# Low parts of up's and gate's left factors subtracted on DVE instead of POOL, with one low part of the operand forms, in a two-layer hybrid trunk

## The chip, the cores and the metric

The kernel runs on one core of a Trainium2 chip. The metric is the device time of one execution in microseconds (us), the median of the runs of a kernel. The engines have the profile's names: PE multiplies matrices, DVE and POOL do elementwise arithmetic, ACT applies functions and copies, SP issues the transfers. Each engine takes its instructions strictly in the order of its own queue.

## What is computed

Two layers over 1024 prompt frames and 64 frames of a running stream (1088 tokens, width 1024). Layer 0 mixes tokens with a state-space model and a gated linear unit, layer 1 with forgetting attention; each is followed by a convolutional feed-forward block. Cut from the reference:

```python
def conv_ffn(x, hist, w_up, w_gate, conv_w, conv_b, w_down):
    a = x @ w_up                                   # 1024 -> 2816
    a_pad = jnp.concatenate([hist.astype(a.dtype), a], axis=1)
    conv = a_pad[:, 0:l] * conv_w[0]
    for j in range(1, CONV_WIDTH):
        conv = conv + a_pad[:, j:j + l] * conv_w[j]
    h = jax.nn.gelu(conv + conv_b) * (x @ w_gate)
    return h @ w_down, a_pad[:, -(CONV_WIDTH - 1):]
```

## The kernel before

Activations stand transposed, as eight tiles of 128 features by 1088 tokens, in chunks of 272 tokens. Every fp32 matrix is split into a high part (a rounded copy, made by ACT) and a low part (the value less its high part), and a product is three matmuls: high by high, high by low, low by high.

Up and gate (`ffn`, `channels`) take the 2816 output features in 11 pairs of 128. For each pair `left_factors` prepares the weights and `seven` multiplies by the Strassen-Winograd scheme: seven products of 12 matmuls for each half of the tokens (a = 0 and 1), accumulated in the PSUM banks A, B, G and H. The first pair of a layer (the **entry**, where `steps` is given) runs up for half 0, gate for both halves and up for half 1, with a third call of `left_factors`; the other ten pairs have two calls. So there are 2 x 23 = 46 calls.

`left_factors` works in this order. A transfer brings `raw` (L296). ACT copies the first 128x1024 half of it to `hi` (L301) and an engine subtracts to make `lo` (L302): these are p1 and p2, called X here. Four sums on POOL (L308 to L311) then overwrite parts of `raw`; L310 and L311 write what X's split reads, and must wait for X's `lo`. Then come Y (p6, p3) and Z (p7, p4), each `hi` and `lo` of 128x1024, and s1 (p5), 128x512 (`s1h`, `s1l`). `seven` uses them in the order p1, p2, p6, p7, p5, p3, p4.

At the entry the operands themselves are still being made: `Norm.to_forms` computes the norm's factor (L164, L165, L179 to L197), scales x (L236) and forms the seven combinations (L255 to L261), each with a high part on ACT (L229) and a low part on POOL or DVE (L230). For half 0 this runs while the layer's mixer (`glu` in layer 0, `wo` with L133 to L135 and L1452 in layer 1) ends; for half 1 it runs between the products of the first call. On DVE, L409 and L415 add the finished banks of up and gate, and free them; L424 is the convolution, L454 multiplies by gate, L456 makes the result's low part. On ACT, L340 copies a bank that is read twice. L123 is another low part, of the other weights, on POOL.

The order on every engine is set by a scheduler which simulates the whole program when it is built. A change of one instruction's engine therefore changes the order of all queues; after that the order is fixed.

Of the kernel before, what the change touches and what calls it, by code (L numbers as in the profile page):

```python
# [9 lines left out]
F32 = mybir.dt.float32  # L10
F32R = mybir.dt.float32r
AF = mybir.ActivationFunctionType
OP = mybir.AluOpType
# [130 lines left out]
class Norm:  # L144
# [10 lines left out]
    def add(self, i, d, fast=False):  # L155
        k = self.k
        nc = k.nc
        o, n = NCH[i]
        x = k.x[d][:, o:o + n]
        if d == 0:  # L160
            nc.scalar.activation(self.s[i], x, AF.Square)
        else:
            q = k.tmp.tile([P, CW], F32, name="tm")[:, :n]
            nc.scalar.activation(q, x, AF.Square)  # L164
            (nc.gpsimd if d % 2 and not fast else nc.vector).tensor_tensor(self.s[i], self.s[i], q, op=OP.add)  # L165
# [50 lines left out]
    def to_forms(self, a, g):  # L216


        k = self.k
        nc = k.nc  # L220
        v = nc.vector
        inv = [self.inverse(i) for i in HALVES[a]]
        yield
        pb = [self.spread(i, r) for i, r in zip(HALVES[a], inv)]
        k.late = []

        def split(j, t, at):
            h, l = (k.form(j, p, a)[:, at:at + 2] for p in range(2))
            nc.scalar.activation(h, t, AF.Copy)  # L229
            (nc.gpsimd if j in (1, 3, 4) else v).tensor_tensor(l, t, h.bitcast(F32), op=OP.subtract)  # L230

        def normed(t, i, th, at):
            o, n = NCH[HALVES[a][th]]
            for d in range(2):
                f = 4 * i + at + d
                v.scalar_tensor_tensor(t[:, d], k.x[f][:, o:o + n], k.gains[:, g, f:f + 1], pb[th], op0=OP.mult, op1=OP.mult)  # L236

        def pair():
            t = k.big.tile([P, T], F32, name="b").rearrange("p (h k c) -> p h k c", h=2, c=CW)
            return t[:, 0], t[:, 1]  # L240

        left = {}
        for at in (0, 2):
            left[at] = b11, b21 = pair()
            normed(b11, 0, 0, at)
            normed(b21, 1, 0, at)
            split(0, b11, at)
            split(1, b21, at)
        for at in (0, 2):
            b11, b21 = left[at]  # L250
            b22, b12 = pair()
            normed(b22, 1, 1, at)
            normed(b12, 0, 1, at)
            split(5, b22, at)
            v.tensor_tensor(b22, b22, b12, op=OP.subtract)  # L255
            split(3, b22, at)
            v.tensor_tensor(b12, b12, b11, op=OP.subtract)
            v.tensor_tensor(b11, b22, b11, op=OP.add)
            split(2, b11, at)
            split(4, b12, at)  # L260
            v.tensor_tensor(b21, b21, b11, op=OP.subtract)  # L261
            if a:
                split(6, b21, at)
            else:
                k.late.append(lambda t=b21, at=at: split(6, t, at))
# [25 lines left out]
def left_factors(k, w, c0):  # L291

    nc = k.nc
    add = nc.gpsimd.tensor_tensor
    raw = k.wraw.tile([P, KT, 2 * P], F32, name="raw")
    nc.sync.dma_start(raw, w[:, c0:c0 + 2 * P].rearrange("(k p) c -> p k c", p=P))  # L296
    a11, a12, a21, a22 = (raw[:, 4 * i:4 * i + 4, P * f:P * f + P] for f in range(2) for i in range(2))

    def split(t, pools, shape, name):
        h, l = (q.tile(shape, F32R, name=name[i]) for i, q in enumerate(pools))  # L300
        nc.scalar.activation(h, t, AF.Copy)  # L301
        add(l, t, h.bitcast(F32), op=OP.subtract)  # L302
        return [[(h[:, 4 * i + kt], l[:, 4 * i + kt]) for kt in range(4)] for i in range(shape[1] // 4)]

    pair = (k.whi, k.wlo), [P, KT, P], ("hi", "lo")
    p1, p2 = split(raw[:, :, 0:P], *pair)
    s1 = k.idle[:, 0:4 * P].rearrange("p (a b) -> p a b", b=P)
    add(s1, a21, a22, op=OP.add)  # L308
    add(a21, a11, a21, op=OP.subtract)
    add(a11, s1, a11, op=OP.subtract)  # L310
    add(a12, a12, a11, op=OP.subtract)  # L311
    p6, p3 = split(raw[:, :, 0:P], *pair)
    p7, p4 = split(raw[:, :, P:2 * P], *pair)
    p5, = split(s1, (k.ws, k.ws), [P, 4, P], ("s1h", "s1l"))
    return p1, p2, p6, p7, p5, p3, p4
# [1260 lines left out]
```

## Time and profile before

| | us |
|---|---|
| median of 3 runs | 2758.65 |
| lowest, highest | 2757.81, 2765.99 |
| the profiled execution | 2759.6 |
| its span, first to last instruction | 2757.8 |
| PE busy | 2632.0 |
| DVE busy | 1563.6 |
| POOL busy | 1466.7 |
| ACT busy | 1071.5 |

Busy time is the sum of an engine's instructions, blocked time within an instruction included. The mean granted clock of TensorE is 0.967 of full speed.

### The profile page before, as it was taken

What the parts mean: (1) busy time and instruction counts of PE and PEld (TensorE: products, weight loads), DVE (VectorE), ACT (ScalarE), POOL (GpSimd) and SP (SyncE); (2) the same over time, 40 slices, a digit from 0 to 9 for tenths busy, and PEclk for the clock granted to TensorE, in tenths of its full rate; (3) what the DMA queues carried; (4) which work ended last, traced back from release to release, by engine and by line L of the source; (5) the groups of instructions that cost most, each with busy time, mean ns of one, the idle gap of its engine ahead of it and who ended that gap; (6) DMA issues with size and microseconds to landing.
All of it is one profiled execution on the core that took longest, in us unless ns stands there. A gap on an engine that the chain in (4) does not pass through costs nothing. (4 is left out here: it accounts for less than half of the span.)

```text
span 2757.8 us, 52693 instructions
## 1 busy us (share of the span) xinstructions
PE 2632.0 (95%) x21030; PEld 2479.0 (90%) x21030; DVE 1563.6 (57%) x2986; ACT 1071.5 (39%) x2134; POOL 1466.7 (53%) x1110
## 2 busy tenths in 40 slices
PE   7987999899999999999999999999889999999998
PEld 4776999899999999999999866669889999999998
DVE  5898235676566633344322288873776666563335
ACT  5553333454444410023222277773344444430013
POOL 4675446786676621235222277764887776742223
PEclk8887999999999999999999999999899999999999
DMA  5123523132332393115685677753223232366211
GB/s 151 40 51 62 155 89 113 47 111 96 110 111 84 130 353 128 49 39 171 178 226 163 189 176 193 191 151 106 76 79 125 81 112 99 107 261 237 87 49 66
DMA packets 262985, 347.41 MB, mean 126 GB/s; under 512 B 32908, under 2 KB 217220, under 8 KB 262740
## 3 DMA queue, kind: packets, MB, share of 16 engines
q1 hardware_dynamic: 262740, 344.04, 40.4%
q8 instruction: 166, 2.72, 0.4%
q14 instruction: 79, 0.65, 0.1%
HBM read 232.37 MB, written 102.56 MB: 121 GB/s over the span
## 5 line engine op out<-in xcount | busy, mean ns | idle before, releaser
L123 POOL TENSOR_TENSOR lo<-raw,hi 128x1024 fp32r<-128x1024 f32 (+2 forms) x127 | 278.3, 2195 | 634.4 <-ACT hi L122 587.6
L302 POOL TENSOR_TENSOR lo<-raw,hi 128x1024 fp32r<-128x1024 f32 x138 | 377.2, 2736 | 208.3 <-ACT hi L301 208.2
L133 PE MATMUL mm<-xh,hi 128*128 128x272 f32 x1664 | 482.8, 291 | 2.7 <-ACT hi L122 1.1
L135 PE MATMUL mm<-xh,lo 128*128 128x272 f32 x1664 | 480.1, 290 | 2.7 <-POOL lo L123 2.7
L134 PE MATMUL mm<-xl,hi 128*128 128x272 f32 x1536 | 444.2, 290 | 0.0
L482 DVE TENSOR_TENSOR x<-x,mm 128x272 f32<-128x272 f32 x448 | 193.1, 436 | 303.2 <-PE mm L135 273.4
L336 PE MATMUL mm<-e,hi 128*128 128x272 f32 x1760 | 344.2, 291 | 7.8 <-ACT tm L340 7.2
L133 PEld LDWEIGHTS mm<-xh,hi 128*128 128x128 f32 x1664 | 315.8, 190 | 3.9 <-DVE tm L1384 1.5
L135 PEld LDWEIGHTS mm<-xh,lo 128*128 128x128 f32 x1664 | 314.6, 190 | 3.4 <-POOL lo L123 3.4
L122 ACT ACTIVATE hi<-raw 128x1024 fp32r<-128x1024 f32 (+2 forms) x127 | 122.9, 972 | 499.5 <-PE mm L134 388.1
L336 PE MATMUL mm<-xh,hi 128*128 128x272 f32 x1408 | 280.3, 293 | 21.9 <-DVE x L409 14.0
L134 PEld LDWEIGHTS mm<-xl,hi 128*128 128x128 f32 x1536 | 291.9, 190 | 0.1
L336 PEld LDWEIGHTS mm<-e,hi 128*128 128x128 f32 x1760 | 278.9, 190 | 8.8 <-ACT tm L340 7.5
L336 PE MATMUL mm<-e,lo 128*128 128x272 f32 x880 | 256.0, 291 | 2.8 <-POOL lo L302 2.8
L336 PEld LDWEIGHTS mm<-xh,hi 128*128 128x128 f32 x1408 | 226.4, 192 | 24.0 <-DVE x L409 14.9
L133 PE MATMUL mm<-e,hi 128*128 128x272 f32 x704 | 206.6, 294 | 11.3 <-issue 10.5
L336 PE MATMUL mm<-xh,lo 128*128 128x272 f32 x704 | 206.3, 294 | 0.0
L336 PE MATMUL mm<-xl,hi 128*128 128x272 f32 x1056 | 205.5, 289 | 0.0
L134 PE MATMUL mm<-e,hi 128*128 128x272 f32 x704 | 204.4, 291 | 0.0
L135 PE MATMUL mm<-e,lo 128*128 128x272 f32 x704 | 202.3, 291 | 0.0
L424 DVE SCALAR_TENSOR_TENSOR x<-x,cw,x 128x1090 f32<-128x1090 f32 x88 | 193.8, 2218 | 12.8 <-ACT x L422 12.0
L301 ACT ACTIVATE hi<-raw 128x1024 fp32r<-128x1024 f32 x138 | 145.0, 1053 | 92.8 <-PE mm L336 79.4
(408 smaller groups left out, 6591.3 us busy)
## 6 DMA issues: line engine op xcount, KB each, us to landing
e<-hD SPq DMA_DIRECT2D x48, 544.0 KB
raw<-in_ffn_w_up SPq DMA_DIRECT2D x24, 1024.0 KB
hD<-b SPq DMA_DIRECT2D x44, 544.0 KB
raw<-in_ffn_w_gate SPq DMA_DIRECT2D x22, 1024.0 KB
hD<-x SPq DMA_DIRECT2D x44, 512.0 KB
raw<-in_ffn_w_down SPq DMA_DIRECT2D x48, 384.0 KB
raw<-in_ssm_w_glu SPq DMA_DIRECT2D x112, 128.0 KB
xh<-hD SPq DMA_DIRECT2D x24, 544.0 KB
```

The lines of the kernel that those rows point to most:

```text
L122: nc.scalar.activation(hi, raw, AF.Copy)
L123: nc.gpsimd.tensor_tensor(lo, raw, hi.bitcast(F32), op=OP.subtract)
L133: mm(ps, h, rh, start=first, stop=False)
L134: mm(ps, h, rl, start=False, stop=False)
L135: mm(ps, l, rh, start=False, stop=last)
L301: nc.scalar.activation(h, t, AF.Copy)
L302: add(l, t, h.bitcast(F32), op=OP.subtract)
L336: nc.tensor.matmul(bank[:, :CW], x, y, start=not more and kt == 0 and i == 0, stop=kt == 3 and i == 2, skip_group_check=True)
L424: v.scalar_tensor_tensor(c, ab[i][:, r:r + T + 2], cw[:, r, f:f + 1], c, op0=OP.mult, op1=OP.add)
L482: v.tensor_tensor(x, x, ps[:, :m], op=OP.add)
```

## The change

Two engine choices: the low parts of X, Y, Z and s1 (L302) go from POOL to DVE, and so does the low part of operand form 3 (L230). The four sums stay on POOL, the high parts on ACT.

```diff
-            (nc.gpsimd if j in (1, 3, 4) else v).tensor_tensor(l, t, h.bitcast(F32), op=OP.subtract)
+            (nc.gpsimd if j in (1, 4) else v).tensor_tensor(l, t, h.bitcast(F32), op=OP.subtract)
...
         nc.scalar.activation(h, t, AF.Copy)
-        add(l, t, h.bitcast(F32), op=OP.subtract)
+        nc.vector.tensor_tensor(l, t, h.bitcast(F32), op=OP.subtract)
```

The scheduler's order moves with it. **First place: POOL at the entry of layer 1**, around the first call (`raw_22792`); `s_21620` is the norm's sum, whose idle columns hold s1. Before:

```order
L308 TENSOR_TENSOR s_21620<-raw_22792 128x512
L165 TENSOR_TENSOR s_21620<-s_21620,tm_22593 128x272
L309 TENSOR_TENSOR raw_22792<-raw_22792 128x4x128
L302 TENSOR_TENSOR s1l_22811<-s_21620,s1h_22810 128x512
L302 TENSOR_TENSOR lo_22795<-raw_22792,hi_22794 128x1024
L165 TENSOR_TENSOR s_21620<-s_21620,tm_22622 128x272
L310 TENSOR_TENSOR raw_22792<-s_21620,raw_22792 128x4x128
L311 TENSOR_TENSOR raw_22792<-raw_22792 128x4x128
```

With the change:

```order
L308 TENSOR_TENSOR s_21620<-raw_22792 128x512
L165 TENSOR_TENSOR s_21620<-s_21620,tm_22593 128x272
L309 TENSOR_TENSOR raw_22792<-raw_22792 128x4x128
L165 TENSOR_TENSOR s_21620<-s_21620,tm_22622 128x272
L310 TENSOR_TENSOR raw_22792<-s_21620,raw_22792 128x4x128
L311 TENSOR_TENSOR raw_22792<-raw_22792 128x4x128
```

The two subtractions between L309 and L310 are gone from POOL; on DVE they now stand between two rows of L1452.

**Second place: DVE in the entry of layer 1**, between the scaling of x for half 1 (L236) and the row that frees the first bank (L409). Before:

```order
L236 SCALAR_TENSOR_TENSOR b_22928<-x7_21613,gains_70,mm_22911 128x272
L236 SCALAR_TENSOR_TENSOR b_22937<-x4_21610,gains_70,mm_22915 128x272
L236 SCALAR_TENSOR_TENSOR b_22937<-x5_21611,gains_70,mm_22915 128x272
L236 SCALAR_TENSOR_TENSOR b_22937<-x0_21606,gains_70,mm_22915 128x272
L236 SCALAR_TENSOR_TENSOR b_22937<-x1_21607,gains_70,mm_22915 128x272
L230 TENSOR_TENSOR xh0_1441<-b_22919,xh0_1441 128x544
L230 TENSOR_TENSOR xh0_1441<-b_22928,xh0_1441 128x544
L409 TENSOR_TENSOR x0_22975<-mm_22829,tm_22827 128x272
```

With the change:

```order
L236 SCALAR_TENSOR_TENSOR b_22928<-x7_21613,gains_70,mm_22911 128x272
L302 TENSOR_TENSOR s1l_23029<-s_21620,s1h_23028 128x512
L236 SCALAR_TENSOR_TENSOR b_22937<-x4_21610,gains_70,mm_22915 128x272
L236 SCALAR_TENSOR_TENSOR b_22937<-x5_21611,gains_70,mm_22915 128x272
L236 SCALAR_TENSOR_TENSOR b_22937<-x0_21606,gains_70,mm_22915 128x272
L236 SCALAR_TENSOR_TENSOR b_22937<-x1_21607,gains_70,mm_22915 128x272
L230 TENSOR_TENSOR xh0_1441<-b_22919,xh0_1441 128x544
L302 TENSOR_TENSOR lo_23021<-raw_23010,hi_23020 128x1024
L230 TENSOR_TENSOR xh0_1441<-b_22928,xh0_1441 128x544
L409 TENSOR_TENSOR x0_22975<-mm_22829,tm_22827 128x272
```

Two low parts of the second call (`raw_23010`) have come into this stretch of DVE, ahead of the row that frees the bank.

**Third place: DVE at the end of layer 1's entry**, where the first pair's convolution runs beside the second pair's first products. Before:

```order
L424 SCALAR_TENSOR_TENSOR x2_23352<-x0_22975,cw1_3648,x2_23352 128x1090 x2
L409 TENSOR_TENSOR x1_22977<-mm_23295,tm_23293 128x272
L409 TENSOR_TENSOR x0_23449<-mm_23436,tm_23419 128x272
L409 TENSOR_TENSOR x0_23449<-mm_23454,tm_23434 128x272
L454 TENSOR_TENSOR x2_23352<-x2_23352,b_23060 128x1024
L454 TENSOR_TENSOR x2_23352<-x2_23352,b_23060 128x64
L424 SCALAR_TENSOR_TENSOR x3_23358<-x1_22977,cw1_3648,x3_23358 128x1090 x2
L456 TENSOR_TENSOR x2_23352<-x2_23352,b_23364 128x1024
```

With the change:

```order
L424 SCALAR_TENSOR_TENSOR x2_23352<-x0_22975,cw1_3648,x2_23352 128x1090 x2
L409 TENSOR_TENSOR x1_22977<-mm_23295,tm_23293 128x272
L302 TENSOR_TENSOR lo_23399<-raw_23384,hi_23398 128x1024
L409 TENSOR_TENSOR x0_23449<-mm_23436,tm_23419 128x272
L409 TENSOR_TENSOR x0_23449<-mm_23454,tm_23434 128x272
L302 TENSOR_TENSOR lo_23623<-raw_23620,hi_23622 128x1024
L454 TENSOR_TENSOR x2_23352<-x2_23352,b_23060 128x1024
L454 TENSOR_TENSOR x2_23352<-x2_23352,b_23060 128x64
L424 SCALAR_TENSOR_TENSOR x3_23358<-x1_22977,cw1_3648,x3_23358 128x1090
L456 TENSOR_TENSOR x2_23352<-x2_23352,b_23364 128x1024
L456 TENSOR_TENSOR x2_23352<-x2_23352,b_23364 128x64
L424 SCALAR_TENSOR_TENSOR x3_23358<-x1_22977,cw1_3648,x3_23358 128x1090
```

Two low parts have come in, and the second L424 of `x3_23358` now stands behind L456. On SP the order changes by one place in a pair: a transfer of up's weights and one of the results change places.

## Rows read from the trace of the kernel before

**Rows 1.** The page, part 1: busy time, share of the span and instructions.
```profile
span 2757.8 us, 52693 instructions
PE 2632.0 (95%) x21030; PEld 2479.0 (90%) x21030; DVE 1563.6 (57%) x2986; ACT 1071.5 (39%) x2134; POOL 1466.7 (53%) x1110
```

**Rows 2.** Windows: both entries by halves, a later stretch of up/gate; us.
```profile
core 0: us, PE busy (x) PEld busy (x) DVE busy (x) ACT busy (x) POOL busy (x), PEclk, DMA share, GB/s
430.00:540.00 110.00, 96.90 (x722) 94.81 (x721) 64.24 (x92) 43.75 (x74) 77.18 (x45) 0.95 0.21 65
540.00:600.00 60.00, 55.36 (x420) 54.27 (x419) 42.53 (x43) 30.17 (x52) 51.68 (x27) 0.97 0.30 100
1960.00:2022.00 62.00, 48.20 (x317) 46.85 (x315) 45.30 (x62) 22.49 (x40) 48.70 (x30) 0.83 0.11 34
2022.00:2070.00 48.00, 42.90 (x323) 42.02 (x322) 32.89 (x37) 25.67 (x43) 42.53 (x21) 0.96 0.29 95
2200.00:2250.00 50.00, 50.00 (x399) 50.00 (x399) 31.25 (x37) 21.24 (x37) 36.97 (x22) 1.00 0.26 88
```

**Rows 3.** PE's waits, 430 to 600 us: total, times, longest, us.
```profile
PE mm L336 <- DVE x L409: 6.9, 2, 4.2
PE mm L336 <- DVE xh L230: 2.6, 1, 2.6
PE mm L336 <- POOL lo L302: 1.4, 2, 0.8
```

**Rows 4.** PE's waits, 1960 to 2070 us.
```profile
PE mm L336 <- DVE x L409: 7.1, 2, 4.2
PE mm L336 <- ACT tm L340: 6.8, 2, 6.2
PE mm L336 <- ACT xh L229: 3.1, 1, 3.1
```

**Rows 5.** Groups by shape, POOL: busy us, mean ns, idle before.
```profile
L302 POOL TENSOR_TENSOR lo<-raw,hi 128x1024 fp32r<-128x1024 f32 x138 | 377.2, 2736 | 208.3 <-ACT hi L301 208.2
L309 POOL TENSOR_TENSOR raw<-raw 128x512 f32<-128x512 f32 x46 | 64.6, 1405 | 2.9
L302 POOL TENSOR_TENSOR s1l<-s,s1h 128x512 fp32r<-128x512 f32 x46 | 60.0, 1304 | 28.4 <-ACT s1h L301 26.9
```

**Rows 6.** The same view, DVE.
```profile
L424 DVE SCALAR_TENSOR_TENSOR x<-x,cw,x 128x1090 f32<-128x1090 f32 x88 | 193.8, 2218 | 12.8 <-ACT x L422 12.0
L454 DVE TENSOR_TENSOR x<-x,b 128x64 f32<-128x64 f32 x44 | 62.9, 1429 | 0.6
L456 DVE TENSOR_TENSOR x<-x,b 128x1024 f32<-128x1024 f32 x44 | 57.3, 1302 | 24.5 <-ACT b L455 24.5
```

**Rows 7.** Timeline of DVE where POOL is mostly idle: start, us.
```profile
2456.33 0.23 DVE L454 TENSOR_TENSOR x<-x,b 128x64 f32<-128x64 f32 x1
...
2466.30 1.23 DVE L456 TENSOR_TENSOR x<-x,b 128x1024 f32<-128x1024 f32 x1 [1.13 <-ACT b L455]
```

**Rows 8.** Timelines at layer 1's entry: POOL, then ACT, then DVE.
```profile
1960.41 2.60 POOL L302 TENSOR_TENSOR lo<-raw,hi 128x1024 fp32r<-128x1024 f32 x1
...
1968.07 2.36 POOL L302 TENSOR_TENSOR lo<-raw,hi 128x1024 fp32r<-128x1024 f32 x1
...
1966.92 1.06 ACT L301 ACTIVATE hi<-raw 128x1024 fp32r<-128x1024 f32 x1 [5.28 <-POOL raw L311]
...
1968.55 2.47 DVE L230 TENSOR_TENSOR xh<-b,xh 128x544 fp32r<-128x544 f32 x1 [2.45 <-ACT xh L229]
```

**Rows 9.** Windows: right behind PE's longest wait.
```profile
1972.00:1984.00 12.00, 11.77 (x55) 11.56 (x56) 4.29 (x15) 2.85 (x7) 10.47 (x9) 0.53 0.29 89
```

**Rows 10.** Timeline of DVE ahead of PE's second wait in layer 1.
```profile
1988.88 4.02 DVE L230 TENSOR_TENSOR xh<-b,xh 128x544 fp32r<-128x544 f32 x2
1992.82 1.12 DVE L409 TENSOR_TENSOR x<-mm,tm 128x272 f32<-128x272 f32 x3
```

**Rows 11.** Timelines at the end of layer 1's entry: DVE, then POOL.
```profile
2043.22 6.93 DVE L424 SCALAR_TENSOR_TENSOR x<-x,cw,x 128x1090 f32<-128x1090 f32 x2
...
2043.18 5.82 POOL L302 TENSOR_TENSOR lo<-raw,hi 128x1024 fp32r<-128x1024 f32 x2
```

## Prediction

> **What bounds the kernel now.** First the page: PE is busy 95% of the span, DVE 57%, POOL 53% [rows 1]. So the elementwise engines matter only where PE waits for them, and the next question is where that is. The windows answer it [rows 2]. In a later stretch of up/gate PE is busy all 50 us at a granted clock of 1.00, with 399 matmuls: 50 / 399 = 0.125 us each. Nothing can be won there; it can only be lost. In the two entries matmuls are missing. At 0.125 us each, 110 us of layer 0's entry would hold 880 and hold 722, so (880 - 722) x 0.125 = 19.8 us are lost; the 60 us behind it hold 420 of 480, 7.5 us. Layer 1: 317 of 496, 22.4 us, and 323 of 384, 7.6 us. Together 57 us, and that is the most that any relief of DVE and POOL in the entries could give back. (The matmuls of the norm are counted as any other, so it is an upper bound.)
>
> Third, who ends those waits. In layer 0, L409 on DVE ends 6.9 us of them in two waits, L230 on DVE 2.6 us, L302 on POOL 1.4 us [rows 3]. In layer 1 it is L409 again with 7.1 us, a bank copy on ACT (L340) with 6.8, and an operand's high part on ACT with 3.1 us [rows 4]. The named engines are mostly the last link only; L302 itself is rarely named. What makes them late is read from the timelines, below.
>
> **What the change moves.** 138 subtractions of 128x1024 and 46 of 128x512 leave POOL: 377.2 + 60.0 = 437 us of its 1467 [rows 1, 5]. What they cost on DVE the trace does not show, since DVE has no L302. The nearest row is L456, a subtraction of the same shape with two operands in SBUF: 1.23 us where POOL stood still, 1.30 us in the mean [rows 6, 7]. I take 1.23, and half of it, 0.62, for the 128x512. The upper bound is POOL's own price, 2.74 and 1.30 [rows 5]. On DVE the whole is then 138 x 1.23 + 46 x 0.62 = 198 us, against 437 removed.
>
> The second effect is that the engines hold each other up. L454's 128x64 takes 0.23 us where POOL is idle and 1.43 us in the mean [rows 6, 7]. At layer 1's entry a 128x544 on DVE takes 2.47 us from 1968.55, while POOL's low part runs from 1968.07 to 1970.43 [rows 8]; by size it should take 544 / 1024 x 1.23 = 0.65 us (an estimate), and it ends 0.6 us after POOL's instruction does. So a DVE instruction with two operands waits until POOL's is done. The two engines' times add up in such a place, and the move shortens their sum, by 437 - 198 = 239 us over the run; none of it counts where PE is full.
>
> **The stretches where PE is full: 0.** A call is 168 matmuls, so 50 us hold 399 / 168 = 2.4 calls. At 3 x 1.23 + 0.62 = 4.3 us a call DVE gains 10.3 us and stands at 31.3 + 10.3 = 41.6 of 50 [rows 2] if nothing that blocks it went away; but POOL gives up 2.4 x 9.5 = 22.8 of its 37 us, so I expect 32 to 38. The cover is these 8 us and more. At POOL's price DVE would stand at 31.3 + 22.8 = 54 of 50, and be the bound.
>
> **Layer 1, first half of the entry: -5.** PE's longest wait, 6.2 us [rows 4], follows back through the bank copy and the L164 ahead of it on ACT to DVE's L230 from 1968.55, which waited 2.45 us for ACT's high part, which waited behind the high part of Y on ACT (1966.92, idle 5.28 us for L311) [rows 8]. In front of L311 POOL did s1l and X's low part, 1.30 + 2.60 = 3.9 us [rows 5, 8]. With the change both are off POOL there, but L310 and L311 still wait for X's low part, now on DVE, and for an L165; I take 2.9 of the 3.9. Behind the wait TensorE ran at 0.53 of its clock for 12 us, mostly at the lower of its two levels, 1.2 GHz [rows 9]: 12 x 0.47 = 5.6 us. A wait half as long should leave some of that; I take 3 (0 to 5.6). Next late is the chain to the first L409, PE's wait of 4.2 us [rows 4]. There s1l and a low part have come in ahead of L409: +1.9 us. Two L230 in that chain take 4.02 us instead of 1.3 [rows 10], so 2.7 us of blocking may shrink; I count 1.4 of it. -2.9 - 3 + 0.5 = -5.4, rounded to -5 (from -10 to +2).
>
> **Layer 0, first half: 0.** The mixer's end is another one, but the two waits (L409 of 4.2 and L230 of 2.6 [rows 3]) come from the same DVE chain: more of its own work, less blocking, as just counted: +1.9 against 1.4 to 2.7 us. I take 0 (from -5 to +4).
>
> **Ends of both entries: -8.5.** Here the first pair's convolution runs on DVE beside the second pair's first products. Two L424 take 6.93 us while POOL's two low parts take 5.82 us [rows 11]; by L456's price for 1090 elements they would take 2.6. In this place the blocking removed is 4.3 us against 2 x 1.23 = 2.5 us added, and there are two such stretches in the end of an entry. So the second L409 waits, 6.9 - 4.2 = 2.7 and 7.1 - 4.2 = 2.9 us [rows 3, 4], should go: -5.6. Layer 0's waits for POOL's low part (1.4 us [rows 3]) become waits for DVE's, half as long: -0.7, and the same in layer 1. Of the 15.1 us lost there, 15.1 - 8.4 = 6.7 are then small waits and reduced clock; a fifth of them goes with the two waits, -1.4. Sum -8.4, rounded to -8.5 (from -13 to +2).
>
> **Form 3: 0.** Eight subtractions of 128x544 cost 0.65 us each on DVE, 5.2 in all, where it is nearly full; POOL's stop blocking it for longer than that. Cover: DVE work in the mixers' ends that PE does not wait for; without it +2.
>
> **Sum.** -5 + 0 - 8.5 + 0 = -13.5. The profiled execution took 2759.6 us, 1.8 more than its span; 2759.6 - 13.5 = 2746.1. The median is 1.0 below the profiled execution: 2745.
>
> **Rivals.**
> *No difference.* In all four stretches the low parts added to DVE's chain cost what the blocking removed gives, and the 2.9 us at layer 1 only make PE wait 2.9 us longer for L409. For it: L409, not POOL, ends the most waits [rows 3, 4]. Against it: 6.93 us for two L424. It gives -3 to +3: about 2758. A rule leads there too: the Perfetto Trace Analysis page of the Trainium skill, "Optimizing Scalar/DVE Operations", warns that work passed between these two engines may not help, because they share a port. The trace agrees with the sharing; whether the conclusion follows, no run has shown.
> *Slower: the in-order chain on DVE.* A low part waits for ACT's high part, and the banks' L409 and L415 wait behind it on DVE. In each of the four stretches that adds the full 1.9 us, and up to 2.6 more where it finds POOL's sums (1.4 us each [rows 5]) in its way; no blocking goes. With 2.5 us each, 4 x 2.5 = 10 us: 2769. It decides once what is added exceeds what is unblocked by about 2 us a stretch. Against it: POOL's part of the lock falls by more than DVE's own work grows. The far end, DVE as the bound at 54 of 50, would cost 4 us in 50 over 20 pairs of 336 x 0.125 = 42 us: 67 us. I give it 2 in 100.
> *More.* Both entries keep their clock, and the L230 waits go too: -25, 2734.
>
> **Chances.** Forecast 0.52, no difference 0.24, slower 0.12, more 0.12. A change within 0.3%, 8 us, can't be told from none. So faster 0.64, same 0.24, slower 0.12. The range takes in no difference, and leaves out most of "slower" and the end of "more": 2728 to 2763.
>
> **What will show it.** L302 on DVE at 1.2 to 1.5 us; L424's mean from 2.2 to below 1.7; the window 2200 to 2250 still at 50.00; layer 1's 6.2 us wait down to about 3; no wait of 2.5 us and more for L409 at the ends of the entries. I am wrong if L302 on DVE takes over 2 us, or if waits for L409 in the first halves grow.

## The result and the profile after

The changed kernel takes 2729.95 us in the median of 4 runs (2729.06 to 2734.30), the kernel before, beside it, 2758.23 (4 runs). The ratio is 0.9895, with a 95% interval from 0.9874 to 0.9917: 1% faster, 28 us, where 13.5 had been forecast, though inside the range given. The profiled execution took 2729.35 us, 30.25 less than the one of before.

The page of the changed kernel, part 1, to be read against [rows 1]:

```profile
span 2727.6 us, 52627 instructions
PE 2617.9 (96%) x21030; PEld 2467.3 (90%) x21030; DVE 1570.5 (58%) x3178; ACT 1079.1 (40%) x2134; POOL 1018.7 (37%) x918
```

POOL lost 448 us, and DVE, with 192 instructions more, is busy only 7 us longer. The groups by shape say why (line, engine, operation, tiles and shapes, count | busy us, mean ns | idle before):

```profile
L302 DVE TENSOR_TENSOR lo<-raw,hi 128x1024 fp32r<-128x1024 f32 x138 | 176.2, 1277 | 31.2 <-ACT hi L301 31.1
L424 DVE SCALAR_TENSOR_TENSOR x<-x,cw,x 128x1090 f32<-128x1090 f32 x88 | 118.9, 1368 | 0.3 <-ACT x L422 0.2
...
L302 DVE TENSOR_TENSOR s1l<-s,s1h 128x512 fp32r<-128x512 f32 x46 | 34.7, 754 | 56.5 <-ACT s1h L301 56.5
...
L454 DVE TENSOR_TENSOR x<-x,b 128x64 f32<-128x64 f32 x44 | 26.5, 602 | 0.1
```

The low parts cost DVE 176.2 + 34.7 = 210.9 us, but L424 alone gives back 193.8 - 118.9 = 74.9 us and L454's 128x64 another 36.4, against [rows 6].

To see where the time came from, the windows are cut at the same matmuls in PE's order, counted from its first: 3550, 3990, 4310, 4750, 7700, and 14900, 15400, 15950. A stage, the stretch between two such cuts, then holds the same number of matmuls in every kernel. Its length less PE's busy time is read as what PE waited, and more busy time for the same matmuls as reduced clock. The windows of the kernel before (start:end and length, then the busy time of each engine, the granted clock of PE behind POOL's; the long stage from 7700 to 14900, between the full stretch and the end of layer 1's mixer, is left out):

```profile
core 0: us, PE busy (x) PEld busy (x) DVE busy (x) ACT busy (x) POOL busy (x), PEclk, DMA share, GB/s
427.07:486.52 59.45, 56.97 (x442) 56.53 (x441) 26.30 (x38) 21.88 (x36) 36.62 (x22) 0.97 0.30 96
486.52:542.11 55.59, 44.97 (x322) 43.32 (x321) 40.84 (x61) 23.65 (x42) 42.66 (x26) 0.94 0.13 39
542.11:604.92 62.81, 58.17 (x442) 57.08 (x441) 46.38 (x46) 30.72 (x52) 52.06 (x26) 0.97 0.31 105
604.92:976.25 371.33, 371.33 (x2952) 371.33 (x2951) 227.84 (x264) 163.68 (x280) 251.71 (x136) 1.00 0.33 116
1940.74:2026.93 86.19, 71.73 (x503) 70.16 (x501) 63.68 (x86) 32.94 (x60) 69.64 (x42) 0.88 0.20 62
2026.93:2102.91 75.98, 71.55 (x553) 70.88 (x551) 52.39 (x58) 38.30 (x63) 63.83 (x32) 0.98 0.31 108
```

And of the changed kernel:

```profile
425.86:481.81 55.95, 55.19 (x443) 54.97 (x442) 33.72 (x41) 21.32 (x36) 32.57 (x19) 1.00 0.32 102
481.81:534.67 52.86, 45.75 (x323) 44.33 (x322) 42.93 (x72) 22.34 (x41) 20.15 (x13) 0.90 0.20 61
534.67:590.11 55.44, 55.44 (x442) 55.39 (x441) 48.95 (x63) 32.99 (x55) 20.50 (x14) 1.00 0.33 114
590.11:961.44 371.33, 371.33 (x2952) 371.33 (x2951) 221.86 (x328) 167.62 (x277) 88.57 (x68) 1.00 0.34 115
1923.72:2003.41 79.69, 69.01 (x502) 67.64 (x501) 65.95 (x101) 32.85 (x58) 39.14 (x26) 0.91 0.24 74
2003.41:2072.73 69.32, 69.32 (x553) 69.25 (x552) 54.70 (x74) 38.59 (x64) 25.79 (x18) 1.00 0.32 111
```

Read the lengths line by line. The fourth, the full stretch, is the same to the hundredth. The ends of the entries (third and sixth) went from 62.81 to 55.44 and from 75.98 to 69.32 us, and PE is now busy in all of both, at a clock of 1.00: nothing is left there. The end of layer 0's mixer (first) gave 3.5 us, the first half of layer 0's entry 2.7, the mixer's end with the first half in layer 1 (fifth) 6.5.

What is left in the fifth is reduced clock, 0.91, and 79.69 - 69.01 = 10.7 us of PE's waits, against 14.5 before. Here are the longest, 1930 to 2060 us, against [rows 4]:

```profile
PE mm L179 <- POOL s L165: 4.5, 1, 4.5
PE mm L336 <- DVE lo L302: 4.1, 1, 4.1
PE mm L336 <- DVE b L415: 1.1, 1, 1.1
PE mm L336 <- ACT hi L301: 1.0, 1, 1.0
```

The 6.2 us wait became one of 4.5, at the same place in PE's order (the 15101st matmul, counted from 0). The 4.2 us wait for L409 did not go: in its place (the 15199th) stands a wait of 4.1 us for a low part on DVE. In layer 0's first half it went the same way, from 4.2 us for L409 to 3.2 for a low part. The timelines of ACT and then DVE show the one in layer 1:

```profile
1965.08 1.06 ACT L301 ACTIVATE hi<-raw 128x1024 fp32r<-128x1024 f32 x1 [0.18 <-PE mm L336]
...
1966.82 1.71 DVE L236 SCALAR_TENSOR_TENSOR b<-x,gains,mm 128x272 f32<-128x272 f32 x4
1968.46 1.71 DVE L230 TENSOR_TENSOR xh<-b,xh 128x544 fp32r<-128x544 f32 x1
1970.09 2.28 DVE L302 TENSOR_TENSOR lo<-raw,hi 128x1024 fp32r<-128x1024 f32 x1
```

The high part is ready at 1966.1, but the low part starts at 1970.09, behind five other instructions of DVE's queue, and takes 2.28 us itself, where the mean is 1.28.

### The profile page after: what moved, and what is told of

Same layout as the page of the kernel before. It is cut to its first block, busy times and chain, and to the rows that moved or that the text cites. A ratio compares the mean times of both kernels' runs of the same rounds, so it can differ in the third digit from the quotient of the medians.

```text
span 2727.6 us, 52627 instructions
## 1 busy us (share of the span) xinstructions
PE 2617.9 (96%) x21030; PEld 2467.3 (90%) x21030; DVE 1570.5 (58%) x3178; ACT 1079.1 (40%) x2134; POOL 1018.7 (37%) x918
## 5 line engine op out<-in xcount | busy, mean ns | idle before, releaser
L123 POOL TENSOR_TENSOR lo<-raw,hi 128x1024 fp32r<-128x1024 f32 (+2 forms) x127 | 279.9, 2208 | 664.8 <-ACT hi L122 553.9
L122 ACT ACTIVATE hi<-raw 128x1024 fp32r<-128x1024 f32 (+2 forms) x127 | 123.0, 972 | 505.0 <-PE mm L134 373.1
L135 PEld LDWEIGHTS mm<-xh,lo 128*128 128x128 f32 x1664 | 313.3, 189 | 2.7 <-POOL lo L123 2.7
L310 POOL TENSOR_TENSOR raw<-s,raw 128x512 f32<-128x512 f32 x46 | 63.3, 1377 | 397.2 <-DVE lo L302 396.0
L340 ACT ACTIVATE tm<-mm 128x272 f32<-128x272 f32 x264 | 102.7, 391 | 248.6 <-PE mm L336 247.5
```

The costliest lines, as they stand in the source:

```text
L122: nc.scalar.activation(hi, raw, AF.Copy)
L123: nc.gpsimd.tensor_tensor(lo, raw, hi.bitcast(F32), op=OP.subtract)
L135: mm(ps, l, rh, start=False, stop=last)
L340: nc.scalar.activation(t, bank[:, :CW], AF.Copy)
```

## Experiments

Lengths of the stages in the profiled executions, from windows cut as above (us):

| kernel | mixer 0's end | layer 0 first half | layer 0 end | full stretch | mixer 1's end, layer 1 first half | layer 1 end |
|---|---|---|---|---|---|---|
| before | 59.45 | 55.59 | 62.81 | 371.33 | 86.19 | 75.98 |
| changed | 55.95 | 52.86 | 55.44 | 371.33 | 79.69 | 69.32 |
| changed, again | 55.96 | 54.34 | 55.46 | 371.33 | 80.85 | 70.07 |
| form3_only | 55.97 | 51.49 | 62.81 | 371.33 | 85.75 | 75.20 |
| low_only | 57.95 | 50.31 | 55.42 | 371.34 | 82.88 | 69.44 |
| first_two | 55.97 | 52.67 | 63.06 | 371.33 | 82.53 | 76.37 |
| not_first_two | 55.94 | 51.35 | 55.43 | 371.34 | 79.32 | 69.60 |
| junk_pool | 55.97 | 53.57 | 66.34 | 396.23 | 84.82 | 81.72 |
| late_junk | 55.97 | 55.29 | 68.17 | 389.94 | 87.02 | 84.58 |
| no_pool | 55.96 | 51.06 | 55.29 | 371.32 | 74.22 | 69.16 |
| no_pool, again | 55.93 | 50.91 | 55.29 | 371.32 | 74.24 | 69.16 |
| y_pool | 55.95 | 54.93 | 55.46 | 371.33 | 82.53 | 69.59 |
| fast_tail | 55.96 | 51.97 | 55.51 | 371.33 | 80.88 | 70.42 |
| all_dve | 55.33 | 50.31 | 55.30 | 371.31 | 79.65 | 69.16 |

The changed kernel's two executions show how far one stage repeats: within 0.8 us at the ends, 1.5 in the first halves. The first halves of the second one, layer 0 and then layer 1:

```profile
481.64:535.98 54.34, 47.19 (x322) 45.78 (x321) 42.71 (x72) 22.34 (x41) 20.14 (x13) 0.87 0.18 59
1926.38:2007.23 80.85, 70.19 (x503) 68.82 (x501) 66.01 (x101) 32.84 (x58) 39.13 (x26) 0.89 0.23 73
```

PE's waits (length less busy) are 7.1 and 10.7 us in both executions; all of the difference is the clock, 0.87 and 0.89 here against 0.90 and 0.91. So a difference in PE's waits can be read more finely than one in a stage's length.

Medians carry more than that: the state-space stage, which none of the edits touches, took some 10 us longer in some executions (last section), so a median with many of those is late by up to that much. What is said of a stage goes by the table. The experiments ran on three chips, each beside the kernel before; their ratios are to that.

**Which of the two edits.** The first kernel moves form 3 alone, the second the factors' low parts alone:

```diff
# form3_only, against the changed kernel
-        nc.vector.tensor_tensor(l, t, h.bitcast(F32), op=OP.subtract)
+        add(l, t, h.bitcast(F32), op=OP.subtract)
# low_only
-            (nc.gpsimd if j in (1, 4) else v).tensor_tensor(l, t, h.bitcast(F32), op=OP.subtract)
+            (nc.gpsimd if j in (1, 3, 4) else v).tensor_tensor(l, t, h.bitcast(F32), op=OP.subtract)
```

> Only form 3's low part is on DVE; all low parts of up's and gate's left factors stay on POOL. Theory (the low parts of the left factors hold DVE up, and the gain is made where they run): the ends of both entries and layer 1's wait of 6.2 us stay as before; only the end of the layer 0 mixer, where the changed kernel gained 3.5 us, may gain up to 3.5. Time 2755 to 2759 us. Rival (the gain is that of a luckier order, which any such edit gives): 5 us and more are gained or lost in places where form 3 has no part.

> Only the low parts of up's and gate's left factors are on DVE; form 3 stays on POOL. Theory: both ends of the entries gain their 14 us together, the first halves 9, so 24 to 27 us in all: 2731 to 2735 us. Rival (form 3 brings part of the entries' gain, because its POOL instructions stood among them): 15 to 20 us, 2738 to 2743.

Measured: form3_only 2756.3 us, ratio 0.9983 (0.9963 to 1.0002), which can't be told from no change; low_only 2734.25, ratio 0.9909 (0.9882 to 0.9936), in the theory's range. The ends of the entries are those of before without the low parts (62.81, 75.20) and those of the changed kernel with them (55.42, 69.44): they are the low parts' alone. In every other kernel of the table but the two with extra work on POOL, too, the ends go by where the later calls' low parts are, whatever else was moved, so they are not the luck of an order.

The end of mixer 0 gains all 3.5 us with form 3 alone, and 1.5 with the low parts alone. In layer 0's first half form3_only gains 4.1 us, where the theory had it at nothing. That is not the rival's case, since two of form 3's low parts for half 1 run there; they were left out of the theory. PE waits 10.6 us in that half before, 8.1 in form3_only, 7.0 in low_only and 7.1 with both: the two edits do not add up.

Form 3 pays through POOL's queue. The timeline of POOL at the end of mixer 0, before:

```profile
432.45 3.17 POOL L230 TENSOR_TENSOR e<-b,e 128x544 fp32r<-128x544 f32 x2 [5.56 <-ACT e L229]
436.46 1.36 POOL L165 TENSOR_TENSOR s<-s,tm 128x272 f32<-128x272 f32 x1 [0.84 <-ACT tm L164]
437.78 4.88 POOL L123 TENSOR_TENSOR lo<-raw,hi 128x1024 fp32r<-128x1024 f32 x2
```

and in form3_only:

```profile
432.66 1.45 POOL L230 TENSOR_TENSOR e<-b,e 128x544 fp32r<-128x544 f32 x1 [6.32 <-ACT e L229]
434.65 2.63 POOL L123 TENSOR_TENSOR lo<-raw,hi 128x1024 fp32r<-128x1024 f32 x1 [0.54 <-ACT hi L122]
437.25 1.25 POOL L165 TENSOR_TENSOR s<-s,tm 128x272 f32<-128x272 f32 x1
```

One of two L230 is gone, and the low part of the mixer's own weights (L123), for which PE waits there, starts 3.1 us earlier. PE's two waits in that stage, 1.1 us for the weights' high part (L122) and 1.4 for L123, become one of 0.8 for L123, and the clock goes from 0.97 to 1.00: 1.7 us are waits, 1.8 clock. Low_only keeps both waits as they were (1.05 and 1.42 us), and yet its clock did not fall. Five microseconds right behind them, before and in low_only:

```profile
442.00:447.00 5.00, 5.00 (x35) 5.00 (x35) 1.13 (x3) 1.01 (x3) 1.38 (x2) 0.81 0.52 157
442.00:447.00 5.00, 5.00 (x43) 5.00 (x41) 1.32 (x3) 1.89 (x3) 1.97 (x3) 1.00 0.49 168
```

So the 1.5 us of low_only in this stage are no wait that the low parts took away.

**Which calls.** The low parts on DVE in the first two calls of a layer only, and in all but these:

```diff
+def left_factors(k, w, c0, first=False):
...
+        (nc.vector if first else nc.gpsimd).tensor_tensor(l, t, h.bitcast(F32), op=OP.subtract)   # first_two
+        (nc.gpsimd if first else nc.vector).tensor_tensor(l, t, h.bitcast(F32), op=OP.subtract)   # not_first_two
...
+                seven(k, left_factors(k, w_up, c0, True), ((0,),), put_up, steps)
+                seven(k, left_factors(k, w_gate, c0, True), ((0,), (1,)), put_gate)
```

> The low parts of the left factors are on DVE only in the first two calls of each layer (up and gate for the first half of the entry), form 3 too; all later ones are on POOL. Theory: what is gained in the entry's first half (2.7 us in layer 0, 6.5 in layer 1, with 3.5 at the mixer's end in layer 0) stays, the ends lose their 14 us again: 2743 to 2747 us. Rival (the ends gain since the first half leaves less work over): the ends keep 5 us and more, 2735 to 2741.

> The low parts of the left factors are on POOL in the first two calls of each layer and on DVE in all later ones; form 3 on DVE. Theory: the ends of the entries keep their 14 us, the first halves lose their 9: 2738 to 2743 us. Rival (in the first halves DVE is now so full that POOL does them as well): as the changed kernel or better, 2726 to 2732.

Measured: first_two 2754.33 us, ratio 0.9984 (0.9967 to 1.0002); not_first_two 2732.8, ratio 0.9914 (0.9881 to 0.9946). The first loses the ends again (63.06, 76.37), as the theory had it, but of layer 1's first half it keeps only 3.7 of 6.5 us (the rest is clock), and its median lies above the theory's range. The second keeps the ends, but it keeps the first halves as well (51.35 and 79.32, within the repeat of the changed kernel or below): here the rival is right. With the low parts of the first two calls on POOL the wait for L409 is back, 3.9 us in layer 1, where the changed kernel waits 4.1 us for a low part; the one is worth the other.

Of PE's waits in layer 1's first half, 14.5 us before, form3_only keeps 14.4, and low_only, first_two, not_first_two and the changed kernel have 10.3 to 10.7. So either group of low parts takes off all that both do. What the later calls' do can be placed: up to its 400th matmul that stage takes 66.26 us in not_first_two as in form3_only, and the last hundred take 13.05 instead of 19.50. That is where the third call's low parts run.

**Blocking, or a shorter way to the factor?** Both kernels keep the low parts on DVE and give POOL work that nobody reads. In junk_pool it repeats each subtraction, behind ACT's high part and among the four sums; in late_junk it stands behind all of a call's own work:

```diff
# junk_pool
         nc.vector.tensor_tensor(l, t, h.bitcast(F32), op=OP.subtract)
+        if again:
+            for i in range(0, shape[1], 4):
+                add(k.junk, t[:, i:i + 4], h[:, i:i + 4].bitcast(F32), op=OP.subtract)
# late_junk
     p5, = split(s1, (k.ws, k.ws), [P, 4, P], ("s1h", "s1l"))
+    if again:
+        for _ in range(7):
+            add(k.junk, k.junk, s1, op=OP.add)
```

`k.junk` is 512 columns of the norm's sum tile that are free in these stretches; `again` is false in a layer's first two calls.

> The changed kernel, and beside each low part of the left factors POOL makes the same subtraction once more into columns that nobody reads (128x1024 as two of 128x512), in all calls but the first two of a layer. So DVE's low parts keep their short path, and POOL has the work of before again. Theory (the ends gained because POOL's subtractions no longer hold DVE up): L424 and L454 become slow again, and the ends lose at least 10 of their 14 us: 2740 to 2752 us. Rival (the ends gained because a low part itself is ready sooner, 1.28 us against 2.74): they keep at least 10 us, 2729 to 2734.

> The changed kernel, and in all calls but the first two of a layer POOL makes seven extra sums of 128x512 that nobody reads, on columns that are free, 7 x 1.3 = 9.1 us a call; that is as much as the low parts took there before (9.5), and nothing on the way to a factor waits for it but what stands behind it on POOL. Theory (the ends gained because POOL's work held DVE up): the ends lose at least 7 of their 14 us. Rival (the ends gained because POOL's work stood in the chain that makes the factors): they keep at least 10 us.

Measured: junk_pool 2809.87 us, ratio 1.0188 (1.0157 to 1.0218); late_junk 2803.29, ratio 1.0162 (1.0133 to 1.0191). Both went the theory's way, junk_pool far past its range of time. In junk_pool the extra work also stands among the sums and so in the chain that makes the factors: ACT's high parts wait 96.3 us in all for the call's last sum (L311; L315 in junk_pool, L312 in late_junk). So it alone would not decide. In late_junk that is 11.8 us, as before the change (11.4). The lines of ACT's high parts, junk_pool and then late_junk:

```profile
L302 ACT ACTIVATE hi<-raw 128x1024 fp32r<-128x1024 f32 x138 | 144.7, 1053 | 117.0 <-POOL raw L315 96.3 <-PE mm L340 11.6 <-issue 6.7
L302 ACT ACTIVATE hi<-raw 128x1024 fp32r<-128x1024 f32 x138 | 145.0, 1053 | 79.2 <-PE mm L340 63.8 <-POOL raw L312 11.8 <-PE mm L134 2.0
```

Late_junk's ends are 12.7 and 15.3 us longer than the changed kernel's, 5.4 and 8.6 longer than before the change. So POOL's work by itself undoes the gain. More groups of late_junk (line numbers are 4 higher than in the kernel before from L424 on, 1 higher at L302):

```profile
L318 POOL TENSOR_TENSOR s<-s 128x512 f32<-128x512 f32 x294 | 611.0, 2078 | 18.5
L303 DVE TENSOR_TENSOR lo<-raw,hi 128x1024 fp32r<-128x1024 f32 x138 | 245.5, 1780 | 24.9 <-ACT hi L302 24.9
L428 DVE SCALAR_TENSOR_TENSOR x<-x,cw,x 128x1090 f32<-128x1090 f32 x88 | 184.1, 2108 | 2.7 <-ACT x L426 2.7
```

The convolution on DVE, which takes 1.37 us in the changed kernel, takes 2.11, nearly the 2.22 of before [rows 6], and the low part 1.78 instead of 1.28; the extra sums take 2.08 us each, where the call's own L309 takes 1.42 in the changed kernel. In the full stretch, where PE never waited, it waits now:

```profile
2200.00:2250.00 50.00, 48.95 (x386) 48.33 (x384) 43.83 (x43) 20.83 (x35) 46.10 (x26) 1.00 0.28 100
```

DVE at 43.8 and POOL at 46.1 of 50 us cost PE 1.05 us. The extra work came out larger than meant, 7 x 2.08 = 14.6 us a call where 9.1 was aimed at, so the size of its effect says nothing of the work that was moved; its direction does.

**What is left.** Four more kernels look at the waits that remain:

```diff
# no_pool: the four sums on DVE too
-    add = nc.gpsimd.tensor_tensor
+    add = nc.vector.tensor_tensor
# all_dve: no_pool, and
-            (nc.gpsimd if j in (1, 4) else v).tensor_tensor(l, t, h.bitcast(F32), op=OP.subtract)
+            v.tensor_tensor(l, t, h.bitcast(F32), op=OP.subtract)
# y_pool: Y's low part on POOL in a layer's first two calls
+    p6, p3 = split(raw[:, :, 0:P], *pair, nc.gpsimd if first else nc.vector)
# fast_tail: in glu and wo
-                norm.add(n, d)
+                norm.add(n, d, d > 5)
```

> The four sums of the left factors go to DVE as well, so POOL has no part in them. Theory (DVE is the full engine in the entries by now): the sums' own time, 4 x 0.65 us a call by size, is more than what their blocking costs; waits come back at the ends, 2732 to 2740 us. Rival (what is left of the waits is blocking by the sums): 2723 to 2727. In the full stretches both expect no change.

> The changed kernel, with Y's low part on POOL in the first two calls of a layer. Theory (PE's waits of 3.2 and 4.1 us for a low part on DVE come from its place in DVE's queue, behind L236 and L230): they shrink to 1 or 2 us, 2723 to 2727 us. Rival (the wait of before for L409, 4.2 us in each layer, lies right behind and comes back): 2728 to 2732.

> The changed kernel, with the norm's last two sums of squares (L165, tiles 6 and 7) on DVE for all token chunks in both mixers, instead of one of them on POOL. Theory (POOL is only the last link of the 4.5 us wait in layer 1; the delay is DVE's, which waits for Y's high part with L1452 behind it): at most 1 us gained, 2728 to 2731 us. Rival (POOL's instruction is the delay): 2 to 4 us gained, 2724 to 2727.

> The changed kernel once more, as the measure for the two behind it: 2728 to 2732 us, with the same matmuls at the same distances as in its first profile outside the state-space stage.

> The four sums on DVE as well, once more. Its first profile gained 5.5 us on the changed kernel in layer 1's entry and 1.8 in layer 0's. Theory (every POOL instruction in the entries holds DVE up for more than the same work costs on DVE): 2721 to 2725 us in the median, 5 to 9 below the changed kernel. Rival (that gain was one of order or chance): within 3 us of the changed kernel.

> The sums on DVE, and the low parts of forms 1 and 4 too (16 subtractions of 128x544): POOL keeps nothing of the operand forms and the factors. Theory (as for the sums): 0 to 3 us less than with the sums alone. Rival (DVE, busy 9.6 to 10 of 10 us in stretches of the changed kernel's entries, is the full engine now): 2 to 6 us more.

The changed kernel, once more, took 2735.09 us in the median of 6 (2729.79 to 2746.2), 3 above the range expected, beside 2756.66 for the kernel before: there 21.6 us are gained, ratio 0.9918 (0.9890 to 0.9945).

Y_pool took 2736.39 us (ratio 0.9930, 0.9905 to 0.9955) and fast_tail 2734.27 (0.9908, 0.9878 to 0.9939); both profiled executions had the longer state-space stage, and both medians lie above both ranges. Y_pool did take the wait for the low part in layer 1 from 4.1 to 0.8 us, but PE's wait ahead of it, for the norm's sum, grew to 5.7; the stage lost 1.7 to 2.8 us against the changed kernel. The rival was nearer, with another wait than the one it named. Fast_tail left that wait for the norm's sum at 4.2 us (4.5 in the changed kernel), now ended by DVE's L165, so POOL's was only its last link, as the theory had it.

No_pool went against the theory: 2729.89 and 2726.68 us (ratios 0.9891, 0.9855 to 0.9927, and 0.9882, 0.9856 to 0.9907), the second 8.4 us below the changed kernel beside it, as its second theory had it, though above that range. Layer 1's first half is 5.5 us shorter than in the changed kernel's first execution, twice to within 0.02 us, layer 0's 1.8; the ends don't grow. Its windows over layer 1's entry:

```profile
1924.11:1998.33 74.22, 67.50 (x502) 65.65 (x501) 65.07 (x114) 33.57 (x58) 21.00 (x13) 0.95 0.25 79
1998.33:2067.49 69.16, 69.16 (x552) 69.16 (x551) 58.18 (x92) 38.69 (x64) 0.00 (x0) 1.00 0.32 111
```

In the first line DVE has 114 instructions against 101 in the changed kernel, yet it is busy 65.07 us instead of 65.95, and the clock is 0.95 instead of 0.91. Of the 5.5 us 4.0 are waits: the one for the norm's sum fell from 4.5 to 1.7 us and the one for the low part from 4.1 to 2.0, so the four sums on POOL were in both. In layer 0's first half PE's waits did not fall (7.5 and 7.6 us, 7.1 in the changed kernel); the 1.8 us there are clock.

Moving forms 1 and 4 too (all_dve, 2727.18 us, ratio 0.9883, 0.9858 to 0.9907) gains 0.6 to 0.8 us in each of layer 0's first two stages and loses 5.4 in layer 1's first half, so by the stages its rival is nearer; in the median it can't be told from no_pool. Of the 5.4 us only 0.8 are waits, the rest is clock, in one execution. By the table's five entry stages no_pool is the best of these, 305.7 us against 313.3 and 316.7 for the changed kernel's two executions, while the intervals of the ratios overlap.

## Why the prediction was right or wrong

The direction, the mechanism (POOL's work holds DVE up, and PE waits for DVE) and most of the place held: 26.8 of the 30.25 us came in the stages of the two entries, and the full stretch gave nothing. The size did not hold, -13.5 against -30 in the profiled execution. Two terms of the sum failed: the ends of the entries, sized too small, and form 3, put at nothing. The rival called "more", given 12 in 100, came nearest, but both entries kept their clock only at the ends, not in the first halves (0.90 and 0.91). Term by term:

- *Price on DVE*: 1.23 and 0.62 us forecast, 1.28 and 0.75 measured. *Full stretch*: 0, measured 0.00. DVE was expected at 32 to 38 of 50 us; the same window has 32.54.
- *Ends of both entries*, -8.5: this is the step that failed most, -14.0 measured (7.4 and 6.7), beyond its own bound of -13. The sum counted the two waits for L409 and half of POOL's, and let four fifths of the other 6.7 us stand as "small waits and reduced clock" (a fifth of 6.7 is 1.3, not 1.4). They were no separate loss: with the blocking gone all waits went, and with the waits the reduced clock, from 0.97 and 0.98 to 1.00. By PE's busy time 9.1 us were waits and 5.0 reduced clock, and all of both came back. Low_only, first_two and not_first_two show the low parts of the later calls as the cause, late_junk POOL's work as the means.
- *Form 3*, 0: -3.5 measured at the end of mixer 0. The step looked for the cost on DVE and its cover, not for what stands behind the instruction on POOL, which was the low part that PE waits for.
- *Layer 0, first half*, 0: -2.7, and -1.2 in the second execution. PE's waits fell by 3.5 us in both, and 0.8 and 2.2 of that went to a lower clock. The chain to L409 was not the draw that was counted: its wait went from 4.2 to 3.2 us and L230's from 2.6 to 1.6.
- *Layer 1, first half*, -5: -6.5 and -5.3. That the sum came near is partly luck, since two misses of opposite sign cancel. The 6.2 us wait fell by 1.6 us instead of 2.9, and was to be down to about 3. The reduced clock gave 2.7 of the 3 us forecast (1.5 in the second execution). The chain to L409 is neither shorter nor longer, as counted, but the wait is now named for a low part behind other instructions of DVE: a new wait of the same length in the old one's place, as the slower rival had it, without its price. The third group of waits, 3.1 us for ACT's high part and smaller ones [rows 4], was left out of the sum and gave another 2.1: two of about 1 us are left.
- Left over are 3.5 us in other stages: 1.2 ahead of mixer 0's end and 2.2 in the long stage between the full stretch and mixer 1's end (964.49 to 962.28 us). The former varies from execution to execution; of the 2.2 the second execution keeps 0.9 (963.61), and whether that is the change's stays open.

The warning of the Trainium skill (Perfetto Trace Analysis, "Optimizing Scalar/DVE Operations"), that passing work between DVE and GpSimd (POOL) might not help as they share a port, did not come true in this direction: the same subtraction takes 1.28 us on DVE instead of 2.74 on POOL, so there is less to share. That the two hold each other up, late_junk shows with the numbers above; that a port is the reason is the page's statement, and no run here shows it.

## What to carry to other kernels

When two engines block each other, look first at the sum of both engines' busy time in the stretch where the matrix engine waits, and ask of each wait there whether it shares the cause before letting it stand. The sum is a lead and not a price: all_dve lowered it by 7 us in layer 1's first half (79.1 against no_pool's 86.1), and PE's waits did not fall. Count the reduced clock behind a wait with the wait, but as a chance: at mixer 0's end the same two waits left the clock at 0.81 in one kernel and at 1.00 in another. Before costing a moved instruction at nothing, look at what stands behind it on the queue it leaves, not only on the one it joins. To place a gain, cut the windows at equal counts of matmuls: full stretches then agree to 0.01 us, and a gain of 1 us shows where medians spread by ten.

## What the runs showed of the hardware

POOL can keep DVE out for much longer than one of its own instructions. In the state-space stage two DVE multiplications take 1.95 us in the kernel before (first line); in the profiled execution of first_two, with the same instructions there, they take 13.59, one of them 12.46:

```profile
71.16 1.95 DVE L888 TENSOR_TENSOR Q<-P,Bst 128x512 f32<-128x512 f32 x2 [4.34 <-PE s L893]
70.20 13.59 DVE L888 TENSOR_TENSOR Q<-P,Bst 128x512 f32<-128x512 f32 x2 [1.84 <-PE s L893]
```

POOL ran without a gap from 70.06 to 82.11 us meanwhile; its first two rows and its last three:

```profile
70.06 2.28 POOL L875 TENSOR_TENSOR WC<-P,Cd 128x576 f32<-128x576 f32 x2
72.30 0.61 POOL L595 TENSOR_TENSOR g<-EE,UU 128x256 f32<-128x256 f32 x1
...
80.92 0.61 POOL L595 TENSOR_TENSOR g<-EE,UU 128x256 f32<-128x256 f32 x1
81.50 0.61 POOL L596 TENSOR_TENSOR g<-EE,UU 128x256 f32<-128x256 f32 x1
82.19 1.06 POOL L597 TENSOR_TENSOR E<-g,g 128x256 f32<-128x256 f32 x1
```

The long multiplication ended at 82.66 us, half a microsecond behind the end of L596, where POOL has its first gap (0.08 us). PE waited 10.4 us for it. Four of the fourteen profiled executions have such a multiplication, of 11.7 to 12.5 us (first_two, the second of no_pool, y_pool, fast_tail), and in the other ten none takes over 2.9. The cut at the 3550th matmul comes at 437.3 to 438.7 us in these four and at 425.2 to 429.8 in the ten, so it explains some 10 us of spread. It is not the kernel's: no_pool's first execution is without it. That it is a turn of arbitration between the two engines is a reading of these rows; no run tried it.
